# The last step of a convolution with max pooling, cut into two half steps in banks of their own

## The chip, the cores and the metric

The kernel runs on one core of a Trainium2 chip. The core has five engines that run side by side, each through its own queue in order: PE (matrix products), DVE (vector), ACT (scalar), POOL (also called GpSimd) and SP (which only issues transfers here). PE writes its sums to PSUM, which has eight banks of 512 fp32 values in each of 128 partitions; DVE and ACT read and write PSUM too, POOL does not. The metric is the time of one execution in device microseconds. The time before is the median of 3 runs, 103.41 us (103.34 to 104.08).

## The reference

A 3x3 convolution with padding 1, from 64 to 128 channels, over 16 images of 64x64, and then a maximum over windows of 2x2:

```python
batch, c_in, h, w, c_out, k = 16, 64, 64, 64, 128, 3
conv[b, co] += weight[co, ci, kh, kw] * x_pad[b, ci, kh:kh+h, kw:kw+w]   # over ci, kh, kw
output[b, c, i, j] = np.max(conv[b, c, i*2:(i+1)*2, j*2:(j+1)*2])
```

## The kernel before, in words

**Tiles.** Two images lie side by side in the 128 partitions (64 channels each), as eight tiles `xb` in bf16 with a row of zeros at the top and the bottom. Every matmul uses only the 64 rows of one image, so that two matmuls, one for each image (`h` = 0 and 1, the two lanes), run in the two halves of the array at the same time. `product` (L241) collects the products of both lanes and issues them in pairs, pass by pass. The work is cut into 32 steps: a step is a quarter of a pair of images, 16 rows of the image, that is R = 8 pairs of rows. One step and one lane fill a bank of 512 values for the upper rows of the pairs (`ta`) and another bank for the lower rows (`tb`).

**Products.** A product is three passes, one for each column of the filter (`taps`, L179): the middle one 8x64 = 512 columns wide, the outer two 8x63 = 504. With g0, g1, g2 the rows of the filter, x0 and x1 the two image rows of a pair, and x-1 and x2 the rows around it, steps come in two types:

- K steps: `ta` gets PA1 = (g2-g1) x1 and PA2 = g0 x-1, `tb` gets PB1 = (g0-g1) x0 and PB2 = g2 x2. What both rows have in common, PR = g1 (x0+x1), is added after the maximum over the two rows. Five products, 15 passes.
- W steps (all but 0, 1, 3, 5, 9 and 15, and so the last one, step 31): P2 = GM e goes into `ta`, with e = x0-x1 and GM = (g0+g2-g1)/2, and ACT copies it to `tb` (SE, `seed`, L339). P0 adds g0 (x1-x-1) to `ta`, P3 adds g2 (x2-x0) to `tb`. After the maximum over tb and -ta comes the common part P1 = GP (x0+x1), GP = (g0+g1+g2)/2. Four products, 12 passes, and a copy.

The sums and differences of rows are made beforehand in bf16: S (x0+x1, L300, on DVE), E (x0-x1, L303) and D (the differences for P0 and P3, L305), the last two on DVE or POOL. An `&` makes the rows of two neighbouring steps in one instruction, a `+` takes the other engine.

**After the products**, for each step and lane: EV (`evac`, L328) copies `ta`, negated in W steps, to SBUF on ACT; MX (`rowmax`, L344) takes the maximum of `tb` and that copy on DVE, in place; P1 or PR is added by PE; OD (`odd`, L351) copies the odd columns to SBUF on ACT; CM (`colmax`, L359) takes the maximum of even and odd columns on DVE and, when both lanes are there, issues the output. `OD+` leaves OD out: CM then reduces both columns in one instruction.

**The order** is written out by hand in `ORDER` (L429): one word for each operation, name, step, lane, and it is issued word by word, so each engine's queue follows it. `BANKS` (L483) names the bank that each start of a sum takes, in that order. An operation waits for whatever it depends on; a bank is guarded as a whole, so that a product that writes to one half of a bank waits for a reader of the other half.

**The start.** While the weights load, eight matmuls on constants (L491) keep PE busy. Then the filter rows are made into blocks (g0, g1, g2, D2, D0 and later GM, GP), each is turned by PE transposes (TD2, TG2, ..., `turn`, L136) and copied back to SBUF (VD2, VG2, ..., `turn_out`, L146) by DVE or ACT; u words (`ring`, L122) copy one slot of a block. X words cast the image's rows, L words (`load`, L315) load rows by POOL's own transfers. Step 0 is done in half steps (F, `first_product`, L256), since its rows arrive in two parts. POOL's work is held behind the DVE instruction on SBUF that stands before it (`on_gpsimd`, L70).

**The end before.** Step 31 is a W step. P2, P0 and P3 are whole, and from EV on everything is done in two halves of four pairs of rows (fourth number in the word: `P1.31.0.1` is the second half of lane 0), both halves in the same two banks. The last words are P1.28.0 and CM.28.0. Outputs behind the last operation of ACT are issued by SP and ACT in turn.

Of the kernel before, what the change touches and what calls it, by code (L numbers as in the profile page):

```python
# [11 lines left out]
def kernel(  # L12
# [9 lines left out]
    nc = tc.nc  # L22
# [59 lines left out]
    def span_of(part=None):  # L82
        return (0, R) if part is None else (0, R // 2) if part == 0 else (R // 2, R)
# [95 lines left out]
    def taps(t, h, m0, rows, start=False, skip=None, span=(0, R)):  # L179
        lo = h * CI  # L180
        i0, i1 = span
        if skip == i0:
            i0 += 1
        if skip == i1 - 1:
            i1 -= 1

        def one(kw):
            o0, o1, c0, c1 = (0, W, 0, W) if kw == 1 else (1, W, 0, W - 1) if kw == 0 else (0, W - 1, 1, W)
            if start and kw == 1:
                unset.discard(t)  # L190
            nc.tensor.matmul(  # L191
                acc[:, t, i0:i1, o0:o1],
                wt[lo : lo + CI, tap_of(m0, kw, h), :],
                rows(lo, i0, i1, c0, c1),
                start=start and kw == 1,
                stop=True,
                skip_group_check=True,
            )

        return [lambda kw=kw: one(kw) for kw in (1, 0, 2)]  # L200
# [11 lines left out]
    def rows_at(s):  # L212
        p, q = place[s]
        return xb[p], 2 * R * q + 1
# [5 lines left out]
    def top(s):  # L220
        return 0 if place[s][1] == 0 else None

    def bottom(s):
        return R - 1 if place[s][1] == NQ - 1 else None

    PRODUCTS = {
        "PA1": lambda s, h: taps(take(ta, s, h), h, D2, of_x(s, 1), start=True),
        "PA2": lambda s, h: taps(ta[s, h], h, G0, of_x(s, -1), skip=top(s)),
        "PB1": lambda s, h: taps(take(tb, s, h), h, D0, of_x(s, 0), start=True),
        "PB2": lambda s, h: taps(tb[s, h], h, G2, of_x(s, 2), skip=bottom(s)),  # L230
        "PR": lambda s, h, *part: taps(tb[s, h], h, G1, step1(row["s", s]), span=span_of(*part)),
        "P2": lambda s, h: taps(take(ta, s, h), h, GM, step1(row["e", s]), start=True),
        "P0": lambda s, h: taps(ta[s, h], h, G0, step2(row["d", s], 0)),
        "P3": lambda s, h: taps(tb[s, h], h, G2, step2(row["d", s], 1)),
        "P1": lambda s, h, *part: taps(tb[s, h], h, GP, step1(row["s", s]), span=span_of(*part)),
# [5 lines left out]
    def product(name, s, h, *part):  # L241
        lanes[h].append((name, s, h, *part))
        while lanes[0] and lanes[1]:
            a, b = (PRODUCTS[n](*args) for n, *args in (lanes[0].popleft(), lanes[1].popleft()))
# [11 lines left out]
    def first_product(k, part):  # L256
# [6 lines left out]
        pair_of_taps(where, s, m0, of_x(s, shift), start, skip, span_of(part))  # L263
# [41 lines left out]
    def row_d(s, alt):  # L305
        row["d", s] = d_pool.tile([128, 2 * R, W], BF16, name="d")
        t, f = rows_at(s)
        engine, note = (nc.vector, on_vector) if alt else (nc.gpsimd, on_gpsimd)
        note(
            engine.tensor_tensor(  # L310
                out=row["d", s], in0=t[:, f + 1 : f + 1 + 2 * R, :], in1=t[:, f - 1 : f - 1 + 2 * R, :], op=SUB
# [16 lines left out]
    def evac(s, h, *part, alt):  # L328
# [3 lines left out]
        if TYPES[s] == "K":  # L332
# [11 lines left out]
    def rowmax(s, h, *part):  # L344
        i0, i1 = span_of(*part)
# [5 lines left out]
    def odd(s, h, *part, alt):  # L351
# [3 lines left out]
        i0, i1 = span_of(*part)  # L355
# [3 lines left out]
    def colmax(s, h, *part, free):  # L359
        i0, i1 = span_of(*part)  # L360
        o = tile_of(ot, o_pool, s, WO, "o")
        t = acc[:, tb[s, h], i0:i1]
        if (s, h) in direct:
            nc.vector.tensor_reduce(  # L364
                out=o[:, h], in_=t.rearrange("p r (w two) -> p r w two", two=2), axis=mybir.AxisListType.X, op=MAX
# [3 lines left out]
        if part == (0,):  # L369
            return  # L370
        made.setdefault(s, []).append(h)
        p, q = place[s]
        dst = out[2 * p : 2 * p + 2, :, q * R : (q + 1) * R, :].rearrange("b c h w -> c b (h w)")
        src = o.rearrange("p b h w -> p b (h w)")
        queue = nc.sync
        if free:
            queue = (nc.scalar, nc.sync)[(free + 1) % 2]
# [28 lines left out]
    for m in PRODUCTS:  # L406
        steps[m] = lambda *args, m=m: product(m, *args)
    either = {
        "GS": outer_sum, "D": row_d, "SE": seed,
# [12 lines left out]
    for m in ("G0", "G1", "G2"):  # L422
# [7 lines left out]
        D2 g2 TD2 TG2 g0 D0 XOa+ g1+ TD0 XEa+ TG0 VD2 GS VD0 VG2 VG0+ uG1+ F.0.0 F.2.0 F.1.0 L.0.49.64 XEb+  # L430
        TG1 XOb+ VG1 F.3.0 L.1.0.17 F.3.1 GM uGM+ GP F.0.1 S.0 X1+ F.1.1 uGP+ F.2.1 EV.0.1 L.1.17.33 PA1.1.0
        TGM X2 X3 EV+.0.0 L.1.33.64 PB1.1.0 MX.0.1 MX.0.0 PA2.1.0 PR.0.0 TGP PA1.1.1 X4 PB1.1.1 PR.0.1 PA2.1.1
        PA1.3.0 PB2.1.0 S.1 VGM+ VGP+ PB1.3.0 PB2.1.1 EV.1.1 EV.1.0 PA1.5.0 OD+.0.1 PA2.3.0 PA1.3.1 CM.0.1
        PB1.3.1 L.2.0.33 OD+.0.0 PA2.3.1 PB2.3.1 CM.0.0 PA2.5.0 MX.1.1 EV.3.1 MX.1.0 L.2.33.64 EV.3.0 S&.3
        PB2.3.0 D+.2 PR.1.1 OD.1.1 PA1.5.1 PB1.5.0 S.2 EV.5.0 MX.3.1 E&.4 PR.3.1 PR.1.0 MX.3.0 L.3.0.64 P2.4.1
        OD.3.1 PB2.5.0 PA2.5.1 SE.4.1 PR.3.0 OD.1.0 CM.1.1 D+.4 P0.4.1 P2.4.0 S.4 P3.4.1 EV.5.1 OD.3.0 E+.6
        MX.5.0 EV.4.1 P2.2.1 SE.4.0 CM.1.0 CM.3.0 CM.3.1 P2.6.1 MX.4.1 PR.5.0 P2.6.0 OD.5.0 SE.2.1 E+.7 P0.4.0
        P3.4.0 P1.4.1 P0.2.1 CM.5.0 D+.6 SE.6.0 EV.4.0 P0.6.0 P3.2.1 SE.6.1 S&.8 S&.7 D+.7 P0.6.1 P3.6.0
        EV.2.1 MX.4.0 EV.6.0 E+.8 MX.2.1 L.4.0.64 MX.6.0 P3.6.1 EV.6.1 OD.4.1 PB1.5.1 PB2.5.1 PA1.9.0 P1.4.0
        CM.4.1 P2.7.0 P1.2.1 P1.6.0 MX.6.1 D.8 OD.4.0 P1.6.1 PA2.9.0 SE.7.0 CM.4.0 MX.5.1 D.10 OD.6.0 OD.2.1  # L440
        P2.7.1 P0.7.0 EV.9.0 CM.2.1 PR.5.1 CM.6.0 P3.7.0 OD+.6.1 P2.8.1 EV.7.0 SE.7.1 P0.7.1 P3.7.1 P2.8.0
        CM.6.1 OD.5.1 MX.7.0 PB1.9.0 CM.5.1 SE.8.0 E&.10 SE.8.1 P0.8.1 P2.10.1 P1.7.0 P3.8.1 EV.7.1 S&.10
        MX.7.1 OD.7.0 L.5.0.64 D.14 P0.8.0 P1.7.1 PB2.9.0 CM.7.0 EV.8.0 P3.8.0 SE.10.1 EV.8.1 MX.9.0 MX.8.0
        P0.10.1 P2.2.0 PR.9.0 SE.2.0 MX.8.1 S&.12 P3.10.1 P1.8.0 OD.7.1 P1.8.1 OD.9.0 PA1.9.1 OD.8.0 PA1.15.1
        PA2.9.1 CM.7.1 P0.2.0 P3.2.0 CM.9.0 EV.10.1 EV.2.0 P2.10.0 CM.8.0 MX.10.1 PA1.15.0 E&+.12 MX.2.0
        P1.2.0 OD.8.1 CM.8.1 SE.10.0 PA2.15.1 PA2.15.0 EV.9.1 OD.2.0 PB1.9.1 D+.13 D+.11 CM.2.0 S&.17 P1.10.1
        D+.12 P2.11.0 EV.15.1 EV.15.0 PB2.9.1 P0.10.0 E+.14 P2.12.1 SE.11.0 EV.10.0 OD.10.1 P3.10.0 P2.11.1
        P0.11.0 MX.9.1 MX.10.0 S&.18 SE.12.1 EV.11.0 PR.9.1 P3.11.0 P0.12.1 P1.10.0 P2.12.0 CM.10.1 SE.11.1
        OD.9.1 MX.11.0 OD.10.0 P3.12.1 CM.9.1 EV.12.1 P1.11.0 P0.11.1 SE.12.0 OD.11.0 E&+.18 CM.10.0 MX.12.1
        P3.11.1 P2.13.0 D+.16 EV.11.1 SE.13.0 P1.12.1 P0.12.0 P3.12.0 D+.19 EV.12.0 OD.12.1 CM.11.0 MX.11.1  # L450
        P2.14.1 CM.12.1 P0.13.0 SE.14.1 P3.13.0 P2.13.1 MX.12.0 EV.13.0 P0.14.1 P2.14.0 P3.14.1 E&+.16 SE.13.1
        EV.14.1 SE.14.0 P1.11.1 P1.12.0 P0.13.1 MX.13.0 P3.13.1 P1.13.0 S&.20 S&.15 OD.13.0 L.6.0.64 MX.14.1
        EV.13.1 CM.13.0 P1.14.1 P2.17.1 P0.14.0 P3.14.0 PB1.15.1 EV.14.0 MX.13.1 PB1.15.0 OD.12.0 D.17 OD.14.1
# [94 lines left out]
```

## Time and profile before

| | before |
|---|---|
| median of 3 runs | 103.41 us (103.34 to 104.08) |
| the profiled execution | 103.55 us |
| its span, from the first instruction to the last | 101.8 us |
| mean granted clock of PE | 0.98 |
| matmuls | 867: 8 on constants, 25 transposes, 834 on L191 |
| transfers | 18.02 MB, 177 GB/s on the mean |

The profile is one execution, taken by the hardware's profiler. Engines are busy while an instruction runs. PE's matmuls overlap: the next one starts before the result of the last is there, so that a matmul's own duration (0.38 us for 512 columns) is longer than the time from one to the next. In the groups, `64*128 64x512` is a matmul with 64 rows of weights, 128 columns of them, over 512 columns. `acc` is the whole PSUM, `d`, `e`, `s`, `ev`, `od`, `o` are the tiles of the operations above, `wq` and `wt` the filter blocks before and after the turn. A time behind `<-` is idle time of the engine just before the instruction, with what ended it.

### The profile page before, as it was taken

The page shows a single profiled execution, that of the slowest core. Times are in us where ns is not written, and L with a number is a line of the kernel's source. Part 1 is how long each engine was busy: PE and PEld are TensorE (multiplying, and loading weights), DVE is VectorE, ACT ScalarE, POOL GpSimd, SP SyncE. Part 2 cuts the span into 40 slices and gives each one's busy share as a digit, 9 for nine tenths or more (in the row PEclk, how much of TensorE's full clock was granted, in tenths as well). Part 3 has the DMA queues.
Part 4 walks back from the last instruction along what each step waited for, and adds up shares of the span by engine and source line. Part 5 has one row for each costly group of instructions (what it writes and reads, how often), then busy time and mean ns, then how long its engine had stood idle before and what let it go on. Part 6 is the DMA issues. An engine that isn't in the chain of part 4 may idle for free.

```text
span 101.8 us, 2430 instructions
## 1 busy us (share of the span) xinstructions
PE 95.1 (93%) x867; PEld 54.5 (54%) x867; DVE 91.7 (90%) x200; ACT 83.3 (82%) x186; POOL 56.7 (56%) x44
## 2 busy tenths in 40 slices
PE   6999999999999999999999999999999999998610
PEld 2477444545566666675565555667565555544300
DVE  3559999999999999999999999899999999999640
ACT  5567647889898979999869999999999899988320
POOL 2072502535986752647597568776678997580000
PEclk9999999999999999999999999999999999999965
DMA  2999999999999999870289790879892350420063
GB/s 44 352 327 179 141 186 199 230 234 222 271 227 169 279 259 214 277 248 6 26 132 202 208 354 13 148 155 176 235 333 95 113 206 1 170 90 0 4 231 125
DMA packets 11035, 18.02 MB, mean 177 GB/s; under 512 B 784, under 2 KB 9104, under 8 KB 10384
## 3 DMA queue, kind: packets, MB, share of 16 engines
q0 software_dynamic: 1584, 7.59, 42.2%
q1 hardware_dynamic: 9296, 10.16, 29.3%
q8 instruction: 6, 0.10, 0.4%
q10 hardware_dynamic: 144, 0.13, 0.4%
q14 instruction: 5, 0.04, 0.1%
HBM read 17.07 MB, written 8.39 MB: 250 GB/s over the span
## 4 chain that ended last, share of the span: by engine, by line
PE 92%; DVE 2%; ACT 1%; issue 0%; DVEq 0%
PE acc L191 87%; PE acc L492 4%; PE acc L140 2%; DVE o L368 1%; ACT od L357 1%; DVE acc L347 1%; DVEq L368 0%; DVEq L347 0%
## 5 line engine op out<-in xcount | busy, mean ns | idle before, releaser
L191 PEld LDWEIGHTS <-wt 64*128 64x128 bf16 x834 | 51.5, 94 | 38.6 <-issue 5.5
L191 PE MATMUL acc<-d,wt 64*128 64x504 bf16 (+1 forms) x312 | 62.6, 377 | 0.0
L191 PE MATMUL acc<-s,wt 64*128 64x504 bf16 (+3 forms) x198 | 45.6, 370 | 1.2 <-DVE o L368 0.5
L347 DVE TENSOR_TENSOR acc<-acc,ev 128x512 f32<-128x512 f32 (+1 forms) x66 | 43.4, 678 | 1.2 <-ACT ev L337 0.5
L191 PE MATMUL acc<-e,wt 64*128 64x512 bf16 (+1 forms) x156 | 39.0, 376 | 0.0
L342 ACT COPY acc<-acc 128x512 f32<-128x512 f32 x52 | 30.5, 587 | 3.4 <-PE acc L191 1.4
L310 POOL TENSOR_TENSOR d<-xb 128x1024 bf16<-128x1024 bf16 x13 | 27.7, 2131 | 6.1 <-PE acc L191 2.2
L337 ACT ACTIVATE ev<-acc 128x512 f32<-128x512 f32 (+1 forms) x53 | 30.7, 591 | 0.5 <-PE acc L191 0.2
L297 POOL TENSOR_TENSOR e<-xb 128x1024 bf16<-128x1024 bf16 (+1 forms) x13 | 21.8, 1680 | 12.1 <-DVE d L310 8.8
L191 PE MATMUL acc<-xb,wt 64*128 64x512 bf16 (+7 forms) x168 | 22.9, 344 | 0.0
L357 ACT COPY od<-acc 128x256 f32<-128x256 f32 (+1 forms) x55 | 19.5, 373 | 4.1 <-PE acc L191 2.7
L368 DVE TENSOR_TENSOR o<-acc,od 128x256 f32<-128x256 f32 (+1 forms) x55 | 21.3, 407 | 1.6 <-PE acc L191 1.1
L316 POOL DMA_DIRECT2D xb<-in_x_dram x11 | 6.2, 562 | 12.1 <-DVE e L297 4.6
L297 DVE TENSOR_TENSOR s<-xb 128x1024 bf16<-128x1024 bf16 (+1 forms) x18 | 11.3, 636 | 0.0
L310 DVE TENSOR_TENSOR d<-xb 128x1024 bf16<-128x1024 bf16 x13 | 8.8, 692 | 0.0
L333 ACT COPY ev<-acc 128x512 f32<-128x512 f32 x11 | 6.3, 592 | 2.7 <-PE acc L191 2.6
L364 DVE TENSOR_REDUCE o<-acc 128x256 f32<-128x512 f32 x11 | 7.4, 686 | 0.1
L492 PE MATMUL acc<-const-bfloat16-1.0 128*128 128x512 bf16 x8 | 3.6, 625 | 0.8 <-PEq L529 0.8
L172 POOL TENSOR_TENSOR gsum<-wraw 128x192 f32<-128x192 f32 x1 | 0.8, 809 | 3.8 <-DVE wq L164 3.8
L140 PEld LDWEIGHTS <-wq 128*128 128x128 bf16 x25 | 2.0, 122 | 1.2 <-DVE wq L397 0.8
L158 DVE COPY wt<-acc 128x512 bf16<-128x512 bf16 (+1 forms) x4 | 1.5, 403 | 1.1 <-PE acc L140 1.1
L140 PE MATMUL acc<-ident,wq 128*128 128x128 bf16 x25 | 2.5, 262 | 0.0
(28 smaller groups left out, 17.5 us busy)
## 6 DMA issues: line engine op xcount, KB each, us to landing
out_dram<-o SPq DMA_DIRECT2D x31, 256.0 KB, 6.3
xb<-in_x_dram POOLq DMA_DIRECT2D x5, 1024.0 KB, 11.0
xb<-in_x_dram POOLq DMA_DIRECT2D x2, 496.0 KB, 9.1
xb<-in_x_dram POOLq DMA_DIRECT2D x1, 528.0 KB, 8.7
ksecond<-in_x_dram SPq DMA_DIRECT2D x1, 512.0 KB, 5.5
kthird<-in_x_dram SPq DMA_DIRECT2D x1, 512.0 KB, 6.2
wraw<-in_weight_dram SPq DMA_DIRECT2D x1, 288.0 KB, 3.0
kfirst<-in_x_dram SPq DMA_DIRECT2D x1, 288.0 KB, 3.2
```

The source lines that it names most:

```text
L140: nc.tensor.transpose(tp[:, (j - lo) * CO : (j - lo + 1) * CO], wq[:, j : j + 2, :].rearrange("a b c -> a (b c)"), ident,)
L191: nc.tensor.matmul(acc[:, t, i0:i1, o0:o1], wt[lo : lo + CI, tap_of(m0, kw, h), :], rows(lo, i0, i1, c0, c1), start=start and kw == 1, sto ...
L297: note(engine.tensor_tensor(out=dst, in0=in0, in1=in1, op=op))
L310: engine.tensor_tensor(out=row["d", s], in0=t[:, f + 1 : f + 1 + 2 * R, :], in1=t[:, f - 1 : f - 1 + 2 * R, :], op=SUB)
L333: (nc.vector.tensor_copy if alt else nc.scalar.copy)(out=dst, in_=src)
L337: nc.scalar.mul(dst, src, -1.0)
L342: (nc.vector.tensor_copy if alt else nc.scalar.copy)(out=acc[:, t], in_=acc[:, ta[s, h]])
L347: nc.vector.tensor_tensor(out=t, in0=t, in1=ev[s][:, h, i0:i1], op=MAX)
L357: nc.scalar.copy(out=dst, in_=acc[:, tb[s, h], i0:i1, 1::2])
L364: nc.vector.tensor_reduce(out=o[:, h], in_=t.rearrange("p r (w two) -> p r w two", two=2), axis=mybir.AxisListType.X, op=MAX)
L368: nc.vector.tensor_tensor(out=o[:, h, i0:i1], in0=t[:, :, 0::2], in1=od[s][:, h, i0:i1], op=MAX)
L492: nc.tensor.matmul(acc[:, n].rearrange("p a b -> p (a b)"), ones[:, 0:128], ones, start=True, stop=True, skip_group_check=True)
```

## The change

Step 31 becomes two half steps, 31 and 32, both on the same quarter of the image. `quarter(s)` gives the place of a step, `span_of(s)` the rows of it: all eight pairs for steps below 31, the first four for 31, the last four for 32. The fourth number in the words is gone.

- Step 31 stays a W step, with all of its products and its copies half as wide.
- Step 32 is done without a common part left for later: `ta` gets PA1, PA2 and PRA, `tb` gets PB1, PB2 and PRB, six products and 18 passes, each half as wide. There is no EV, MX or OD for it; CM.32 takes the maximum over both banks and both columns in one reduction.
- Steps 31 and 32 have banks of their own, and so has each lane.
- The output of a step is issued when both lanes are there, now for step 28 too, whose lanes went out one by one. The last output is the first half of the quarter, 128 partitions x 2 images x 128 values, on ACT's queue.
- The order of all words is new, and so is the string of banks, 139 starts instead of 135. At the start D2 is DVE's second instruction, VD2, VG1 and VGM go to ACT, XEa and the sum g0+g2 (GS) to DVE, the turn of G1 comes ahead of that of D0, and the loads of the second pair come ahead of the last rows of the first. Of 26 D words DVE does 8 instead of 13, POOL 18 instead of 13; of the E words DVE does 8 instead of 3, POOL 8 instead of 13.

```diff
+    def quarter(s):
+        return min(s, N - 1)
+
+    def half_of(part):
+        return (0, R // 2) if part == 0 else (R // 2, R)
+
+    def span_of(s):
+        return (0, R) if s < N - 1 else half_of(s - (N - 1))
...
-    def taps(t, h, m0, rows, start=False, skip=None, span=(0, R)):
+    def taps(t, h, m0, rows, start=False, skip=None, span=(0, R), whole=True):
...
+    def first_taps(where, s, h, m0, rows):
+        return taps(take(where, s, h), h, m0, rows, start=True, span=span_of(s), whole=s < N - 1)
...
+        "PA1": lambda s, h: first_taps(ta, s, h, D2, of_x(s, 1)),
+        "PA2": lambda s, h: taps(ta[s, h], h, G0, of_x(s, -1), skip=top(s), span=span_of(s)),
+        "PRA": lambda s, h: taps(ta[s, h], h, G1, step1(row["s", quarter(s)]), span=span_of(s)),
+        "PB1": lambda s, h: first_taps(tb, s, h, D0, of_x(s, 0)),
+        "PB2": lambda s, h: taps(tb[s, h], h, G2, of_x(s, 2), skip=bottom(s), span=span_of(s)),
+        "PRB": lambda s, h: taps(tb[s, h], h, G1, step1(row["s", quarter(s)]), span=span_of(s)),
...
     def seed(s, h, alt):
+        i0, i1 = span_of(s)
         t = take(tb, s, h)
         assert t not in unset
-        (nc.vector.tensor_copy if alt else nc.scalar.copy)(out=acc[:, t], in_=acc[:, ta[s, h]])
+        (nc.vector.tensor_copy if alt else nc.scalar.copy)(out=acc[:, t, i0:i1], in_=acc[:, ta[s, h], i0:i1])
...
-    def colmax(s, h, *part, free):
-        i0, i1 = span_of(*part)
+    def colmax(s, h, free):
+        i0, i1 = span_of(s)
         o = tile_of(ot, o_pool, s, WO, "o")
         t = acc[:, tb[s, h], i0:i1]
+        if s == N:
+            a, b = sorted((ta[s, h], tb[s, h]))
+            nc.vector.tensor_reduce(
+                out=o[:, h, i0:i1],
+                in_=acc[:, a : b + 1 : b - a, i0:i1].rearrange("p k r (w two) -> p r w k two", two=2),
+                axis=mybir.AxisListType.XY,
+                op=MAX,
+            )
...
-        if s == LAST:
-            queue.dma_start(out=dst[:, h : h + 1], in_=src[:, h : h + 1])
-        elif len(made[s]) == 2:
-            queue.dma_start(out=dst, in_=src)
+        queue = (nc.sync, nc.sync, nc.scalar)[free % 2 + 1 if free else 0]
+        queue.dma_start(out=dst, in_=o[:, :, i0:i1].rearrange("p b h w -> p b (h w)"))
...
     ORDER = """
-        D2 g2 TD2 TG2 g0 D0 XOa+ g1+ TD0 XEa+ TG0 VD2 GS VD0 VG2 VG0+ uG1+ F.0.0 F.2.0 F.1.0 L.0.49.64 XEb+
-        TG1 XOb+ VG1 F.3.0 L.1.0.17 F.3.1 GM uGM+ GP F.0.1 S.0 X1+ F.1.1 uGP+ F.2.1 EV.0.1 L.1.17.33 PA1.1.0
+        g2+ g1 D2 g0 TG2 TD2 uG1+ XOa+ TG1 VD2+ VG2 D0 XOb+ GS+ XEa XEb+ X2 TD0 L.1.0.17 TG0 VD0 L.1.17.33
+        VG0+ F.0.0 GP uGP+ F.2.0 F.0.1 F.3.1 GM F.1.0 S.0 X1+ F.1.1 EV+.0.1 EV.0.0 F.3.0 F.2.1 VG1+ uGM+
...
-        P3.30.0 P1.30.1 P0.31.0 EV.30.0 MX.30.0 OD+.30.1 SE.31.1 EV.31.0.0 CM.30.1 P0.31.1 P3.31.1 EV.31.0.1
-        P3.31.0 EV.31.1.0 P1.29.1 MX.31.0.0 P1.30.0 MX.31.0.1 MX.31.1.0 EV.31.1.1 P1.31.0.0 MX.31.1.1 OD.30.0
-        OD.31.0.0 OD.29.1 P1.31.1.0 CM.31.0.0 CM.30.0 P1.31.0.1 OD.31.0.1 OD.31.1.0 P1.31.1.1 P1.28.0 CM.29.1
-        CM.31.1.0 CM.31.0.1 OD.31.1.1 OD.28.0 CM.31.1.1 CM.28.0
+        CM.26.1 MX.29.0 P2.30.1 P1.27.0 P2.29.1 P1.29.0 EV.28.1 CM.27.1 SE.28.0 OD.27.0 E+.31 MX.28.1 CM.27.0
+        OD+.29.0 SE.30.1 P1.28.1 CM.29.0 P0.28.0 P0.30.1 P2.30.0 EV.28.0 P3.28.0 OD+.28.1 P3.30.1 SE.29.1
+        P0.29.1 P2.31.0 P3.29.1 CM.28.1 SE.30.0 EV.30.1 EV.29.1 P0.30.0 D+.31 S&.30 P3.30.0 P2.31.1 MX.28.0
+        EV.30.0 SE.31.0 MX.30.1 MX.29.1 P1.28.0 P1.30.1 MX.30.0 P0.31.0 SE.31.1 OD.28.0 P0.31.1 P3.31.1
+        CM.28.0 P3.31.0 P1.29.1 EV.31.0 P1.30.0 MX.31.0 PB1.32.0 PA1.32.1 EV.31.1 OD.30.1 CM.30.1 PB1.32.1
+        P1.31.0 PRA.32.1 PA1.32.0 PB2.32.0 OD.30.0 PRB.32.0 MX.31.1 OD.31.0 OD.29.1 PRB.32.1 CM.30.0 PB2.32.1
+        CM.31.0 PA2.32.1 PRA.32.0 CM.29.1 P1.31.1 PA2.32.0 CM.32.1 CM.32.0 OD.31.1 CM.31.1
     """
```

More of the change, by code (lines that the diff above doesn't have):

```diff
@@ L189, in one @@
             if start and kw == 1:
-                unset.discard(t)
+                (unset.discard if whole else unset.add)(t)
             nc.tensor.matmul(
@@ L220, in top @@
     def top(s):
-        return 0 if place[s][1] == 0 else None
+        return 0 if place[quarter(s)][1] == 0 else None
     def bottom(s):
-        return R - 1 if place[s][1] == NQ - 1 else None
+        return R - 1 if place[quarter(s)][1] == NQ - 1 else None
+    def first_taps(where, s, h, m0, rows):
+        return taps(take(where, s, h), h, m0, rows, start=True, span=span_of(s), whole=s < N - 1)
     PRODUCTS = {
-        "PA1": lambda s, h: taps(take(ta, s, h), h, D2, of_x(s, 1), start=True),
@@ L228 @@
[L228 to L233, printed above, removed]
@@ L236, with product @@
+        "P1": lambda s, h: taps(tb[s, h], h, GP, step1(row["s", quarter(s)]), span=span_of(s)),
     }
     lanes = (deque(), deque())
-    def product(name, s, h, *part):
-        lanes[h].append((name, s, h, *part))
+    def product(name, s, h):
+        lanes[h].append((name, s, h))
         while lanes[0] and lanes[1]:
-            a, b = (PRODUCTS[n](*args) for n, *args in (lanes[0].popleft(), lanes[1].popleft()))
+            a, b = (PRODUCTS[n](s_, h_) for n, s_, h_ in (lanes[0].popleft(), lanes[1].popleft()))
@@ L262, in first_product @@
             take(where, s, 1)
-        pair_of_taps(where, s, m0, of_x(s, shift), start, skip, span_of(part))
+        pair_of_taps(where, s, m0, of_x(s, shift), start, skip, half_of(part))
     pair_tiles = {}
@@ L310, in row_d @@
             engine.tensor_tensor(
[L311 removed]
+                out=row["d", s][:, 0:n, :], in0=t[:, f + 1 : f + 1 + n, :], in1=t[:, f - 1 : f - 1 + n, :], op=SUB
             )
@@ L349, with odd @@
     direct = set()
-    def odd(s, h, *part, alt):
+    def odd(s, h, alt):
         if alt:
@@ L406 @@
     for m in PRODUCTS:
-        steps[m] = lambda *args, m=m: product(m, *args)
+        steps[m] = lambda s, h, m=m: product(m, s, h)
     either = {
-        "GS": outer_sum, "D": row_d, "SE": seed,
+        "GS": outer_sum, "D": row_d, "SE": seed, "EV": evac, "OD": odd,
         "XOa": lambda alt: cast_first(1, MID, alt),
@@ new lines @@
+        L.2.0.33 S.1 L.2.33.64 OD+.0.1 PA2.1.1 CM.0.1 EV.1.0 PB2.1.1 S.3 PB1.3.1 PA1.3.0 PB1.3.0 MX.1.0
+        PA1.3.1 EV.1.1 OD.0.0 L.3.0.64 PA2.3.0 TGM MX.1.1 PR.1.1 PR.1.0 CM.0.0 PB2.3.1 PA2.3.1 S.2 OD.1.1
+        PB2.3.0 D+.2 E&.2 CM.1.1 VGM EV.3.0 OD+.1.0 TGP P2.4.1 PA1.5.0 CM.1.0 MX.3.0 PA1.5.1 PB1.5.0 EV.3.1
+        PA2.5.1 PA2.5.0 PR.3.0 SE.4.1 MX.3.1 D.4 VGP+ P0.4.1 PB2.5.0 P2.2.1 S.4 P3.4.1 EV.5.0 P2.4.0 PR.3.1
+        S.5 E&.6 S&.7 EV.5.1 EV.4.1 OD.3.0 P2.6.0 SE.2.1 MX.5.0 L.4.0.64 CM.3.0 PR.5.0 SE.4.0 P0.2.1 P3.2.1
```

132 lines of the change are left out of this document (59 added, 73 removed).

## The prediction

> **What bounds the kernel now.** I read the page's head first, then busy time by stretches, then the chain of waits, and last the groups with shapes kept apart.
>
> ```profile
> span 101.8 us, 2430 instructions
> ...
> PE 95.1 (93%) x867; PEld 54.5 (54%) x867; DVE 91.7 (90%) x200; ACT 83.3 (82%) x186; POOL 56.7 (56%) x44
> ```
> ```profile
> 40.00:50.00 10.00, 10.00 (x93) 6.26 (x90) 10.00 (x20) 9.53 (x22) 5.95 (x4) 1.00 0.46 150
> ```
>
> Shares over the span would say that PE has 7% to give. The stretch says otherwise: in a stage of 10 us PE and DVE are both busy for all of it and ACT for 9.53. So the middle is full, and what is not full lies at the two ends. The chain shows them (start, length, what, how many):
>
> ```profile
> 4.35 1.58 PE acc L140 x16
> ...
> 7.25 1.75 PE acc L191 x30
> 9.00 0.44 PE acc L140 x6
> 9.44 82.12 PE acc L191 x747
> ...
> 94.80 0.28 ACT od L357
> ...
> 95.10 0.30 DVE o L368
> ...
> 95.44 0.53 PE acc L191 x6
> ...
> 96.45 0.63 PE acc L191 x3
> ```
>
> Up to 91.56 the chain is PE alone. From about 93.5 it hops between engines: passes, odd columns, column maximum, passes again. The row by row view gives the edges of the full part and the end:
>
> ```profile
> 9.37 1.68 PE L191 MATMUL acc<-xb,wt 64*128 64x512 bf16 x13
> ```
> ```profile
> 93.36 0.38 PE L191 MATMUL acc<-d,wt 64*128 64x504 bf16 x1
> ...
> 97.18 1.32 DVE L368 TENSOR_TENSOR o<-acc,od 128x128 f32<-128x128 f32 x4 [1.12 <-PE acc L191]
> ```
>
> PE's last full pass starts at 93.36; the last DVE result is there at 97.18 + 1.32 = 98.50; the span ends 3.3 us later (issue of the output, landing, closing barrier). These three stretches are my terms: head, stream, tail.
>
> **The change, part by part.**
>
> *Tail, what goes.* Before, both halves of step 31 share a bank, so P1 of the second half cannot start while the first half is read. The waits say so:
>
> ```profile
> PE acc L191 <- DVE o L368: 0.5, 1, 0.5
> PE acc L191 <- DVE acc L347: 0.4, 1, 0.4
> PE acc L191 <- ACT od L357: 0.3, 1, 0.3
> ```
>
> From 93.36 to 98.50 are 5.14 us, in which PE has only three more products to issue (18 passes; 0.65 for one with a full lane, 0.33 for halves, 1.6 together). After, step 32 has banks 6, 4, 1 and 3, whose last readers are EV.31.0, CM.30.1, EV.31.1 and CM.28.0; none is the other half.
>
> *Stream, what is added.* Step 31 had 18 full matmuls and 12 half ones. Now there are 24 half ones for step 31 and 36 for step 32: 30 matmuls more, all half. The two row lanes run together, so I count pairs. Before, 128 full products in pairs lie between 9.37 and 93.36, three passes each: 383 steps in 83.99 us, 0.2193 a step, with the small stalls of this order in it. Without a stall it is (1.68 - 0.38) / 6 = 0.217, by the row at 9.37, whose 13 matmuls are six steps on two lanes and the first of the next. Half passes are those of the first step: the chain's 30 in 1.75 us are 0.117 a pair with some gaps, and half of 0.217 is 0.109; I take 0.11. From start to result one takes 0.27:
>
> ```profile
> L191 PE MATMUL acc<-xb,wt 64*128 64x252 bf16 x28 | 2.4, 270 | 0.0
> ```
>
> In the new order 127 pairs of products are paced by a full lane (two mix a full one with a half one) and 9 are half on both lanes. 381 x 0.2193 = 83.55 and 27 x 0.11 = 2.97, together 86.52. I keep the stalls of before in it, 383 x (0.2193 - 0.217), some 1 us: both orders alternate the same kinds of steps with the same eight banks, and DVE's work after the head is about equal (two half maxima and five D fewer; five E, two reductions and some smaller ones more). That is the largest unknown; bounds below.
>
> *Head.* D2 is now DVE's second instruction, VD2 goes to ACT, three transposes of G1 come ahead of TD0, and GS leaves GpSimd. Rows of before:
>
> ```profile
> 4.16 0.49 DVE L398 TENSOR_TENSOR wq<-wraw 128x192 bf16<-128x192 f32 x1
> 4.98 0.41 DVE L158 COPY wt<-acc 128x512 bf16<-128x512 bf16 x1
> 5.74 0.76 DVE L158 COPY wt<-acc 128x512 bf16<-128x512 bf16 x2 [0.35 <-PE acc L140]
> ```
> ```profile
> 5.37 0.59 ACT L156 COPY wt<-acc 128x512 bf16<-128x512 bf16 x1
> ```
>
> The second turn is read at 5.37 before; D2's takes that place now, so VD2 is 5.37 to 5.96 and F.0.0 starts at 5.98; before, the chain goes on with it at 4.35 + 1.58 = 5.93. Three transposes (0.1 each, 1.58 / 16) put VD0 from 5.74 to about 5.95, done 6.36, so F.2.0 starts at 6.40. Seven products at 0.34 follow without a TG1 or a wait between: 8.78. TGM and TGP (0.44 in the chain) come later and still count: 9.22 stands against 9.37, a gain of 0.15. If VD2 is late by one ACT instruction, it is a loss of 0.3; if F.2.0 does not wait, a gain of 0.35.
>
> *New tail.* Stream end 9.22 + 86.52 = 95.74. The last pass starts 0.11 earlier and takes 0.27, so PE's last result is there at 95.90. What runs behind it:
>
> ```profile
> L364 DVE TENSOR_REDUCE o<-acc 128x256 f32<-128x512 f32 x11 | 7.4, 686 | 0.1
> L347 DVE TENSOR_TENSOR acc<-acc,ev 128x256 f32<-128x256 f32 x4 | 1.6, 430 | 0.2
> L337 ACT ACTIVATE ev<-acc 128x256 f32<-128x256 f32 x4 | 1.3, 381 | 0.2 <-PE acc L191 0.2
> ```
>
> CM.32.1 reads as many elements as the reduction of L364 (two banks of 256 for 512) and its banks are done one product earlier, at 95.6; 0.69. DVE starts an instruction some 0.08 before the one ahead of it is over (4.16 to 4.98 above holds two of 0.49), so CM.32.0 runs 96.2 to 96.9, and CM.31.1 (0.30) 96.8 to 97.1. OD.31.1 (0.28, from 95.9) is hidden by CM.32.0; without that cover it would stand on the path itself. Nothing in the trace reduces across two banks: its price lies between 0.43 (a 256 instruction, if both banks came side by side) and 1.37 (twice 0.69); I take 0.69, the row with the same count. Only one of the two lies on the path, so -0.3 to +0.9. The cover of P1.31.0: counted from the start of P0.31, P0.31 and P3.31 are there at 0.5 and 0.8, EV.31.0 (0.38) ends at 0.9 and MX.31.0 (0.43) at 1.3, and its place in PE's order is 1.64 (two half products and a full one, 0.33 + 0.33 + 0.65, and PB1.32): 0.3 of slack. PA1.32.0 stands a third of a microsecond later and waits for CM.30.1, which follows MX.31.0 and OD.30.1 on DVE and is over at 1.8. Thin, but positive; if the first is gone, P1.31 waits and all behind it with it.
>
> The last transfer keeps its size, in 256 pieces of 512 B instead of 128 of 1 KB:
>
> ```profile
> out_dram<-o ACTq DMA_DIRECT2D x1, 128.0 KB, 2.2
> ```
>
> No row has such pieces on this path. Shorter than before it cannot be, since the bytes are the same and the pieces more; twice the pieces at the same price each would at most add 1.1, half of the 2.2 again, as if all of it were pieces. I leave the 3.3 us as they are, since the bytes stay.
>
> *Work moved between DVE and GpSimd.* Five D's go from DVE to GpSimd, and five e's come back. Each engine's sum changes by under 1.5 us, but they must not meet:
>
> ```profile
> 34.03 0.79 DVE L297 TENSOR_TENSOR s<-xb 128x1024 bf16<-128x1024 bf16 x1
> ```
> ```profile
> 32.12 2.14 POOL L310 TENSOR_TENSOR d<-xb 128x1024 bf16<-128x1024 bf16 x1
> ```
> ```profile
> L347 DVE TENSOR_TENSOR acc<-acc,ev 128x512 f32<-128x512 f32 x62 | 41.7, 694 | 1.0 <-ACT ev L337 0.5 <-PE acc L191 0.2
> L310 POOL TENSOR_TENSOR d<-xb 128x1024 bf16<-128x1024 bf16 x13 | 27.7, 2131 | 6.1 <-PE acc L191 2.2
> L368 DVE TENSOR_TENSOR o<-acc,od 128x256 f32<-128x256 f32 x51 | 20.3, 416 | 0.2
> L297 DVE TENSOR_TENSOR s<-xb 128x1024 bf16<-128x1024 bf16 x14 | 9.6, 697 | 0.0
> L297 POOL TENSOR_TENSOR e<-xb 128x512 bf16<-128x512 bf16 x6 | 6.9, 1160 | 7.9 <-DVE d L310 6.7 <-DVE s L297 1.1
> ```
>
> S&.12 started 0.23 before D.14 was over and took 0.79, where its group needs 0.70: a meeting cost 0.1. The Trainium skill, SBUF — State Buffer, section "Who interferes with whom", speaks for more: a DVE instruction with two SBUF inputs and a GpSimd instruction that reads SBUF exclude each other for the whole instruction, whoever is first. By that rule one early meeting would put up to GpSimd's whole 2.1 us on the sum; the trace shows only this late meeting, which neither proves nor denies it. By the row a meeting is worth 0.1, less than I can count here, and I add nothing.
>
> **Sum.** 97.1 + 3.3 = 100.4 of span. Around the span lie 103.55 - 101.8 = 1.75, so 102.1 for a profiled run; that run was 0.14 above the median of 103.41, so 102.0.
>
> **Rivals.**
>
> *No stalls* (0.15). The new order drops the 1 us of stalls kept in the stream, and the head gains its 0.35 instead of 0.15. For: the stretch shown has no PE idle at all, so the stalls are an accident of places. 102.0 - 1.2 = 100.8.
>
> *The gain goes into the middle* (0.16). GpSimd gets a chain behind S&.27: D.29, D.28, E.30, D.30, E.31, that is 3 x 2.13 + 2 x 1.16 = 8.7 us, and DVE has 8.3 of work until its next instruction on SBUF (eight of 0.694, three of 0.686 and five of 0.416, each less 0.08). Counted from the start of P0.31: MX.30.0 starts at -0.5 and DVE has 11.6 us of work from S&.27 to there, so S&.27 is over at -11.4 and D.28, second in the chain, at -7.1. Its product P0.28 stands eleven pairs before P0.31, 11 x 0.65 = 7.1: no room at all. If the chains come late by 0.6 each (this one and the one of 8.5 us behind E&.18), PE waits for them: 102.0 + 1.2 = 103.2. Against: before has a chain of four behind S&.28, 7.6 us against 6.7 of DVE's work, and its stream still came out at 0.2193.
>
> *The end is not as short* (0.08). Reduction at twice the price and slow pieces: +0.9; 102.9.
>
> *Slower* (0.11). DVE's S, E and D meet GpSimd early and are shut out whole. Two meetings of 2.1 us, at the two chains over 8 us (behind E&.18 and behind S&.27), on a DVE that has no idle time in the stretch shown, reach PE undiminished: 106.2. It decides from 2.4 us on. Against: the mean of this kind over all fourteen is 0.697. This is the rule of the Trainium skill's page on SBUF named above, and no row here shows it.
>
> My forecast has 0.50.
>
> **How the numbers follow.** One per cent is about what a measurement of this kernel can tell from no change; the bounds are 102.4 and 104.4. Of the forecast's 0.50 some 0.40 lie below 102.4 (0.4 of room against the head's 0.3 and the reduction), the rest between. Faster 0.40 + 0.15 = 0.55; within 1% 0.10 + 0.16 + 0.08 = 0.34; slower 0.11. The range goes from 100.9, which cuts half of the no-stall case, to 104.0, which cuts the slower one: just under 0.2 outside.
>
> **What would show it.** First full pass about 8.8, with the two turns after it. PE's last pass near 95.6, no wait of PE on DVE or ACT over 0.2 in the last 4 us. Reductions of 128x128 out at 0.69. From PE's last result to DVE's last 1.2 us. Wrong it is if the full pairs take over 0.2193 us a step, and the releaser then names which rival: "DVE d", "POOL d" or "POOL e" for the GpSimd chain, S, E or D of DVE over 0.8 us for the meetings.

## The result and the profile after

| | before | after |
|---|---|---|
| median of 20 runs each | 103.85 us (103.24 to 104.54) | 103.33 us (102.77 to 104.15) |
| the profiled execution | 103.55 us | 103.78 us |
| its span | 101.8 us | 102.0 us |
| matmuls | 867 | 897 |

The ratio of the times is 0.9947, with a 95% interval of 0.9921 to 0.9972: half a per cent faster, where I had forecast 1.4%. The profiled execution of the changed kernel is one of its slower ones, 0.45 us over its median, so I profiled the same kernel once more (run after_again below) before I counted in tenths. First the profile that came with the result. The head of its page, and the same stretch of 10 us as before (span of the stretch, PE, PE's weight loads, DVE, ACT, POOL, granted clock, DMA share, GB/s):

```profile
span 102.0 us, 2471 instructions
...
PE 95.7 (94%) x897; PEld 59.5 (58%) x897; DVE 91.2 (89%) x199; ACT 82.3 (81%) x182; POOL 56.7 (56%) x43
```
```profile
40.00:50.00 10.00, 10.00 (x92) 5.04 (x90) 9.80 (x19) 9.35 (x21) 6.37 (x5) 1.00 0.96 201
```

PE is still busy for all of it. DVE, which had no gap here before, now has 0.20. The chain of waits of the changed kernel (start, length, what, how many):

```profile
1.19 4.70 DMA kfirst<-in_x_dram
5.90 0.02 issue
5.92 0.41 ACT xb L401
6.33 0.49 ACT wt L162
...
16.86 80.13 PE acc L197 x749
96.99 0.02 issue
97.01 1.29 DVE o L378 x2
98.30 0.20 DVEq L555
```

Two things are to be seen. The tail that hopped between PE, DVE and ACT is gone: PE alone leads up to 96.99, then come the two reductions. And at the other end the chain begins with the first rows of the image: they landed at 5.89 (before 4.43), ACT cast them at 5.92 and only then copied the turned block at 6.33. That is XOa standing ahead of VD2 in ACT's queue. The last operations on DVE, and what SP waited for in all (line, releaser: sum, times, longest), the last two rows being the closing barrier on L555:

```profile
95.36 1.00 DVE L389 TENSOR_TENSOR o<-acc,od 128x256 f32<-128x256 f32 x3
97.01 1.29 DVE L378 TENSOR_REDUCE o<-acc 128x128 f32<-128x512 f32 x2 [0.65 <-PE acc L197]
98.22 0.28 DVE L389 TENSOR_TENSOR o<-acc,od 128x128 f32<-128x128 f32 x1
```
```profile
SPq L396 <- DVE o L389: 75.5, 25, 11.2
SPq L396 <- DVE o L385: 7.0, 5, 2.4
SPq L555 <- DMA out_dram<-o: 1.5, 2, 1.2
SPq L555 <- PEq L555: 1.1, 2, 0.5
```

PE's last result is there at 96.98, since its last row in the trace is this one:

```profile
96.71 0.27 PE L197 MATMUL acc<-s,wt 64*128 64x252 bf16 x1
```

DVE stood idle for 0.65 and began CM.32.1 at 97.01, behind PE's last result of all; forecast was a start 0.3 ahead of it. And in the barrier SP waited 1.1 us; before, the same two rows were these:

```profile
SPq L543 <- DMA out_dram<-o: 1.8, 2, 1.4
...
SPq L543 <- SPq L543: 0.4, 1, 0.4
SPq L543 <- PEq L543: 0.2, 1, 0.2
```

Together 2.6 us after and 2.4 before, though the last transfer itself lands sooner. In the trace's records of semaphores one step of POOL in this barrier, from its first record there to its next, takes 0.44 after and 0.08 before.

### The profile page after: what moved, and what is told of

The parts are those of the page before. It is cut to its first block, busy times and chain, and to the rows that moved or that the text cites. A ratio compares the mean times of both kernels' runs of the same rounds, so it can differ in the third digit from the quotient of the medians.

```text
span 102.0 us, 2471 instructions
## 1 busy us (share of the span) xinstructions
PE 95.7 (94%) x897; PEld 59.5 (58%) x897; DVE 91.2 (89%) x199; ACT 82.3 (81%) x182; POOL 56.7 (56%) x43
## 4 chain that ended last, share of the span: by engine, by line
PE 88%; DMA 5%; DVE 1%; ACT 1%; SPq 0%; issue 0%; DVEq 0%
PE acc L197 88%; DMA kfirst<-in_x_dram 5%; DVE o L378 1%; PE acc L146 1%; ACT wt L162 0%; ACT xb L401 0%; SPq L81 0%; DVEq L555 0%
## 5 line engine op out<-in xcount | busy, mean ns | idle before, releaser
L197 PEld LDWEIGHTS <-wt 64*128 64x128 bf16 x864 | 56.2, 94 | 33.1 <-issue 4.2
L197 PE MATMUL acc<-d,wt 64*128 64x504 bf16 (+3 forms) x312 | 63.4, 373 | 0.0
L322 POOL TENSOR_TENSOR d<-xb 128x1024 bf16<-128x1024 bf16 x18 | 38.1, 2129 | 17.1 <-DVE s L308 9.0
L197 PE MATMUL acc<-s,wt 64*128 64x504 bf16 (+3 forms) x204 | 47.2, 367 | 0.0
L197 PE MATMUL acc<-e,wt 64*128 64x512 bf16 (+2 forms) x156 | 38.2, 372 | 0.0
L355 ACT COPY acc<-acc 128x512 f32<-128x512 f32 (+1 forms) x52 | 29.6, 576 | 3.5 <-PE acc L197 2.3
L197 PE MATMUL acc<-xb,wt 64*128 64x504 bf16 (+6 forms) x192 | 27.2, 333 | 0.5 <-ACT wt L162 0.5
L308 POOL TENSOR_TENSOR e<-xb 128x512 bf16<-128x512 bf16 (+1 forms) x8 | 12.2, 1523 | 5.3 <-PE acc L197 2.7
L308 DVE TENSOR_TENSOR e<-xb 128x1024 bf16<-128x1024 bf16 (+1 forms) x8 | 5.2, 649 | 0.0
L322 DVE TENSOR_TENSOR d<-xb 128x1024 bf16<-128x1024 bf16 (+1 forms) x8 | 5.2, 647 | 0.0
```

Source lines behind the costliest of these rows:

```text
L197: nc.tensor.matmul(acc[:, t, i0:i1, o0:o1], wt[lo : lo + CI, tap_of(m0, kw, h), :], rows(lo, i0, i1, c0, c1), start=start and kw == 1, sto ...
L308: note(engine.tensor_tensor(out=dst, in0=in0, in1=in1, op=op))
L322: engine.tensor_tensor(out=row["d", s][:, 0:n, :], in0=t[:, f + 1 : f + 1 + n, :], in1=t[:, f - 1 : f - 1 + n, :], op=SUB)
```

## The experiments

My theory after the result had two places in it, both small: the wait of CM.32.1, and the closing step. A rival was that the new order of the middle costs PE what the end saves, and another that the head (a cast ahead of the turned block) does. Eleven runs told them apart; the first four on one chip, the others on a second one, each beside the kernel before.

**e1_banks: other banks at the end.** CM.32.1 reads banks 1 and 3 in one instruction. Bank 2 between them belongs to lane 1 of step 31, and its P1.31.1 is PE's very last product. The two SE of step 31 exchange their banks, so that bank 5 is the one that is late, and OD.31.1 goes ahead of CM.32.0:

```diff
-        ... PA2.32.0 CM.32.1 CM.32.0 OD.31.1 CM.31.1
+        ... PA2.32.0 CM.32.1 OD.31.1 CM.32.0 CM.31.1
-        "745632071634025674123706153427601526314"
+        "745632071634025674123706153427601256314"
```

> The changed kernel with SE.31.0 and SE.31.1 in each other's banks (5 and 2), and OD.31.1 ahead of CM.32.0. Theory A (a wait on a bank that lies between the two banks of the reduction): CM.32.1 starts 0.3 us before PE's last result instead of 0.03 behind it, DVE is done 1.2 us behind PE instead of 1.5, and the time falls by 0.35 us, to 0.991 of before where the changed kernel is 0.995. Rival (the reduction waits for its own passes, and the bank between them is no matter): CM.32.1 still starts behind PE's last result, ratio 0.995.

Measured: 103.25 us, ratio 0.9951 (0.9919 to 0.9982). The operations of DVE at the end, and PE's last matmul:

```profile
94.91 1.00 DVE L389 TENSOR_TENSOR o<-acc,od 128x256 f32<-128x256 f32 x3
96.24 1.32 DVE L378 TENSOR_REDUCE o<-acc 128x128 f32<-128x512 f32 x2 [0.33 <-PE acc L197]
97.47 0.28 DVE L389 TENSOR_TENSOR o<-acc,od 128x128 f32<-128x128 f32 x1
```
```profile
96.26 0.27 PE L197 MATMUL acc<-s,wt 64*128 64x252 bf16 x1
```

Now the reduction starts 0.29 before PE's last result (96.24 against 96.26 + 0.27 = 96.53), and DVE ends 1.22 behind PE instead of 1.52. So the wait was for the bank between the two that are read, not for the data: 0.3 us. (OD.31.1 stands behind CM.32.1 in either order and has no part in this wait.) The exchange is not free: ACT's copies for step 31 (SE) now start 0.12 to 0.15 later, counted from the first full pass, and PE's last result comes 0.12 later. From the first full pass to DVE's end the four profiles with the old banks (the changed kernel twice, e2, e6) take 88.94 to 88.96 us, the three with the exchanged banks (e1, e12, e7) 88.76 to 88.78. So 0.18 of the 0.3 reaches the end. The time alone does not show so small a step here, and the expected 0.991 did not come.

**e2_turn_first: the cast behind the turned block.** XOa+ moves behind VD2+ on ACT.

```diff
-        ... TD2 uG1+ XOa+ TG1 VD2+ VG2 ...
+        ... TD2 uG1+ TG1 VD2+ XOa+ VG2 ...
```

> The changed kernel with XOa+ behind VD2+ on ACT instead of ahead of it. Theory A (the cast waits for the first rows, and the copy of the turned weights waits behind it): where the first rows land at 5.9 us as in the profile of the changed kernel, F.0.0 starts at 6.35 instead of 6.87 and the time falls by 0.5 us, to 0.990 of before; where they land at 4.4 as in the profile of before, F.0.0 starts at 6.2 instead of 6.0 and 0.2 us is lost. Rival (the middle is full on DVE as on PE, so a head start is lost in stalls): F.0.0 is earlier but PE's last pass stands where it stood, ratio 0.995.

Measured: 103.31 us, ratio 0.9971 (0.9941 to 1.0). Here the first rows landed early, at 4.44, and ACT's row shows what the move costs then:

```profile
5.40 0.58 ACT L162 COPY wt<-acc 128x512 bf16<-128x512 bf16 x1 [0.51 <-PE acc L146]
5.88 0.41 ACT L401 CAST xb<-kfirst 128x256 bf16<-128x256 f32 x1
```

The cast now waits for the turn and the first product starts at 6.34; in either order the one behind waits for the one ahead. Nothing is won on the mean.

**e12_both: both edits.**

```diff
-        ... TD2 uG1+ XOa+ TG1 VD2+ VG2 ...
+        ... TD2 uG1+ TG1 VD2+ XOa+ VG2 ...
-        ... CM.32.1 CM.32.0 OD.31.1 CM.31.1
+        ... CM.32.1 OD.31.1 CM.32.0 CM.31.1
-        "745632071634025674123706153427601526314"
+        "745632071634025674123706153427601256314"
```

> Both edits of the two runs before. Theory A: the two places are far apart in time, so the two gains add, 0.35 + 0.5 = 0.85 us with late rows, ratio 0.987, and 0.15 us with early ones, 0.994. Rival (full middle): 0.995 or, if only the end counts, 0.991.

Measured: 103.31 us, ratio 0.9953 (0.9919 to 0.9987); DVE again ends 1.22 behind PE, span 101.4. The two together are no more than the first.

**e5_tail_alone: the new end on the old order.** Order and banks of the kernel before up to P3.30.0, and behind it the two half steps, with neighbouring banks for step 32 (3 and 4, 6 and 7), so that none lies between:

```diff
-        P3.30.0 P1.30.1 P0.31.0 EV.30.0 ... CM.31.1.1 CM.28.0
+        P3.30.0 P1.30.1 P1.28.0 EV.30.0 MX.30.0 OD+.30.1 SE.31.1 OD.28.0 P0.31.0 P0.31.1 P3.31.1 P3.31.0 CM.28.0
+        CM.30.1 EV.31.0 P1.30.0 P1.29.1 MX.31.0 EV.31.1 PB1.32.0 PA1.32.1 PB1.32.1 P1.31.0 PRA.32.1 PA1.32.0
+        PB2.32.0 OD.30.0 PRB.32.0 MX.31.1 OD.31.0 OD.29.1 PRB.32.1 CM.30.0 PB2.32.1 CM.31.0 PA2.32.1 PRA.32.0
+        CM.29.1 P1.31.1 PA2.32.0 CM.32.1 OD.31.1 CM.32.0 CM.31.1
```

> The old order and the old banks up to step 30, with the new end alone: step 31 as half step, step 32 with 18 passes and one reduction, in banks of their own (3 and 4, 6 and 7, none in between). Theory A (the end was worth what the prediction said, and the new head gave part of it back): PE starts P0.31 at about 92.3, DVE is done about 5.1 us later, 1.1 us earlier than before: ratio 0.989, better than the changed kernel. Rival (the 30 added half passes eat the gain of the end, and the new order earned the rest): 1.000, worse than the changed kernel.

Measured: 102.55 us, ratio 0.986 (0.9808 to 0.9912), clear of e1 on the same chip (0.9919 to 0.9982). The end alone gives what I had forecast for the whole. Its rows of the end and of the barrier:

```profile
96.30 1.29 DVE L378 TENSOR_REDUCE o<-acc 128x128 f32<-128x512 f32 x2 [0.26 <-PE acc L197]
97.50 0.28 DVE L389 TENSOR_TENSOR o<-acc,od 128x128 f32<-128x128 f32 x1
```
```profile
SPq L551 <- DMA out_dram<-o: 1.5, 4, 0.6
...
SPq L551 <- SPq L551: 0.4, 1, 0.4
SPq L551 <- PEq L551: 0.2, 1, 0.2
```

The reductions start ahead of PE's last result (96.59) here too, and the barrier takes 2.1 us, not 2.6. In this kernel POOL still makes the sum g0+g2 (GS); in the changed one DVE does, and POOL's program is three records shorter (74 against 77 in the trace; GS accounts for two of them, as e8 shows below). That made the next theory: the closing step depends on POOL's program, not on its work.

**after_again: the changed kernel once more**, with no edit.

> The changed kernel once more, on the same chip as the three that follow. With first rows that land at 4.4 to 5.0 us, as in four of the five profiles of this start so far, F.0.0 starts at 5.9 and the first full pass at 9.0, DVE is done at 98.1 and the span is 101.6: closing of 3.5 us behind DVE's last result, against 3.3 and 3.1 in the two profiles of the old order. Ratio 0.995. Rival (late rows are what is usual here): first full pass at 9.5 again and a span of 102.

Measured: 102.95 us, ratio 0.9928 (0.9897 to 0.996), span 101.2. Its chain of waits:

```profile
0.78 3.57 PE acc L506 x8
4.35 1.93 PE acc L146 x19
6.28 7.19 PE acc L197 x90
...
16.07 80.13 PE acc L197 x749
96.20 0.02 issue
96.23 1.29 DVE o L378 x2
```

The long piece is the same to the hundredth, 80.13 for 749 passes, and everything is 0.79 earlier. So what was slow in the first profile lay ahead of the first full pass (9.54 there, 8.77 here): the rows landed at 5.89 there and at 5.00 here, and with them came the cast that the turned block stands behind.

**e6_filler: POOL's program longer by three instructions.** Three memsets of one column each, into a tile that nobody reads, right behind the constants at the start:

```diff
+    spare = const.tile([128, 4], FP32)
+    for n in range(3):
+        nc.gpsimd.memset(spare[:, n : n + 1], 0.0)
```

> The changed kernel with three memsets of 128x1 on GpSimd at the start, into a tile that nobody reads, so that GpSimd's program is as long as before or a little longer. Theory A (one step of the closing barrier on GpSimd takes 0.42 us instead of 0.08 where its program is shorter than before, since its last instructions then lie otherwise in what is fetched): the step takes 0.08 again, the closing falls by 0.35 us, ratio 0.9915. Rival (the step depends on the order of the work or on the last transfers): still 0.42, ratio 0.995.

Measured: 102.99 us, ratio 0.9908 (0.9874 to 0.9942). The barrier:

```profile
SPq L558 <- DMA out_dram<-o: 1.5, 3, 0.7
...
SPq L558 <- SPq L558: 0.4, 1, 0.4
SPq L558 <- PEq L558: 0.2, 1, 0.2
```

2.1 us instead of 2.6, POOL's step 0.08 instead of 0.42, and 3.18 us from DVE's end to the span's end instead of 3.48. More instructions at the start, less time at the end: the profile shows that the step depends on what stands in POOL's program, though the times of the two kernels alone (102.95 and 102.99) would not.

**e7_banks_filler: e1 and e6 together.**

```diff
-        ... CM.32.1 CM.32.0 OD.31.1 CM.31.1
+        ... CM.32.1 OD.31.1 CM.32.0 CM.31.1
-        "745632071634025674123706153427601526314"
+        "745632071634025674123706153427601256314"
+    for n in range(3):
+        nc.gpsimd.memset(spare[:, n : n + 1], 0.0)
```

> The changed kernel with the exchanged banks of step 31 and OD.31.1 ahead of CM.32.0, and the three memsets. Theory A: both gains, 0.3 us at the reduction and 0.35 us in the closing, ratio 0.988 to 0.989. Rival: the time does not follow the profile's end, 0.995.

Measured: 102.48 us, ratio 0.9886 (0.984 to 0.9931), span 100.4. With both repairs the new order gains 1.1%, near the forecast. On this chip that is 0.5 us off the changed kernel, as 0.18 from the banks and 0.3 from the close would have it; the intervals still overlap, but the profile shows both steps: 97.26 to 100.44 at the close, 1.22 from PE to DVE. That its span is the forecast 100.4 to the tenth is luck: its first full pass stands at 8.48, 0.3 earlier than was forecast.

**e8_tail_gs: e5 with the sum on DVE.**

```diff
-        ... XEa+ TG0 VD2 GS VD0 VG2 VG0+ ...
+        ... XEa+ TG0 VD2 GS+ VD0 VG2 VG0+ ...
```

> The old order with the new end alone, and the sum g0+g2 on DVE instead of GpSimd, as the changed kernel has it: GpSimd's program is one operation shorter. Theory A: the step of the closing barrier takes 0.42 us as in the changed kernel and the span is 0.35 us longer than the 100.9 of the new end alone; ratio 0.9895 where the new end alone had 0.986. Rival: the step stays at 0.08, ratio 0.986.

Measured: 102.01 us, ratio 0.9827 (0.9794 to 0.986), the lowest of all. So the expected 0.42 did not come: POOL's step stayed at 0.08 with 75 records; between 74 and 75 it changes. Whether GS was worth a third of a per cent I then asked by itself.

**e9_before_gs: the kernel before, with that one word changed**, and with it **e5_again** and **e8_again**, the two kernels once more, without an edit:

```diff
-        ... XEa+ TG0 VD2 GS VD0 VG2 VG0+ ...
+        ... XEa+ TG0 VD2 GS+ VD0 VG2 VG0+ ...
```

> The kernel before with the sum g0+g2 on DVE instead of GpSimd and nothing else. Theory A (the new end earns what the old order with it shows; this edit only fills a pause of 0.35 us that DVE has there): 1.000 of before, at most 0.2 us faster by the first load of GpSimd leaving earlier. Rival (the head of the changed kernel is what earns, by this part of it): 0.996 or less.

> The old order with the new end alone, a second time. Theory A: 0.986 again, DVE done 1.2 us behind PE's last result and a closing of 3.1 to 3.2 us. Rival (the first measurement was a lucky one and the end is worth no more than the whole change): 0.993.

> The old order with the new end and the sum on DVE, a second time, beside the new end alone on the same chip. Theory A: the sum on DVE is worth 0 to 0.2 us, so 0.984 to 0.986, and this or the run beside it is the fastest of all versions. Rival (the sum on DVE is worth the 0.5 us that lay between their first measurements): 0.981 beside 0.986.

Measured: e9 103.71 us, ratio 1.0015 (0.9983 to 1.0047); e5 again 102.24 us, 0.9876 (0.9836 to 0.9916); e8 again 102.29 us, 0.9881 (0.9844 to 0.9919). GS is worth nothing that the times show, and e8's first 0.9827 was not found again. (In the profiles e8 is 0.2 us shorter than e5 from the first full pass to P0.31, both times, and 0.1 longer in the close.) What stands is that the new end on the old order, in four measurements between 0.9827 and 0.9881, beats both kernels of this case, and that the new order of head and middle adds nothing to it.

**What the middle costs.** From the starts of the products in the traces I took the stretch from the first full pass to P0.31, without the two turns in it. The changed kernel has 126 pairs of products there in 82.97 us, 0.6585 a pair (0.2195 a pass); before had 125 in 82.19, 0.6575 (0.2192); e5 126 in 82.65 and e8 in 82.44. Against before, the new order is neutral to 0.1 us; against the same end on the old order it costs 0.3 to 0.5 us. The waits of PE's weight loads hint at where, first in the first profile of the changed kernel, then in e5_again:

```profile
PEld L197 <- ACT acc L355: 1.2, 4, 0.3
...
PEld L197 <- DVE o L389: 0.4, 1, 0.4
PEld L197 <- ACT ev L349: 0.3, 1, 0.3
```
```profile
PEld L197 <- DVE d L322: 0.3, 1, 0.3
PEld L197 <- DVE wt L164: 0.3, 1, 0.3
PEld L197 <- DVE o L389: 0.2, 1, 0.2
```

In the new order it is the copies of SE on ACT, four times, that PE stands behind; the loads run ahead, so the 1.2 us are more than PE itself loses. I made no run that moves these copies, so that they are the cause of the 0.3 to 0.5 is read from the waits and not shown.

## Why the prediction was wrong in size

The time lies in the range and the direction held, but 0.5% was measured where 1.4% was said. Two steps failed: the start of the last reductions and the closing barrier. The table loses 0.8 of the forecast 1.4 us; the 0.6 that are left agree with the measured half per cent. By steps, forecast against the second profile of the changed kernel, times from the span's start:

| step | forecast | measured | late by then |
|---|---|---|---|
| first full pass | 8.78 | 8.77 | 0.0 |
| two turns behind it | 0.44 | 0.55 | 0.1 |
| P0.31, 126 pairs at 0.2193 a pass | 92.1 | 92.27 | 0.2 |
| PE's last result | 95.90 | 96.19 | 0.3 |
| DVE's last result | 97.1 | 97.71 | 0.6 |
| span | 100.4 | 101.2 | 0.8 |

*Head, stream: right in size, in part by luck.* The full pass came at the time said in this profile. In the five profiles with this head it came between 8.48 and 9.54, 8.90 on the mean, and with the 0.55 of the two turns that is 9.45. The six profiles with the old head (three of them with GS on DVE), which have their two turns ahead of the first full pass, have 9.21 to 9.86 and 9.49 on the mean. So the forecast 0.15 of the head does not show. The stalls kept in the stream came in the size that was kept, 0.2195 a pass against 0.2193, though this was called the largest unknown. By the letter of the prediction's own sign (over 0.2193) that is too much, by 0.1 us in all, and the releaser is ACT's SE, which no rival had named. In the first profile the head was 0.8 later, because XOa+ stands ahead of VD2 and the rows came late; the bounds of the head (-0.3 to +0.35) did not hold that, since I had bounded VD2 by one ACT instruction and not by the landing that the instruction waits for.

*New tail: the first step that failed.* The words "its banks are done one product earlier, at 95.6" took the two banks that CM.32.1 reads. The program guards the range from the first to the last, and the bank between them was PE's last. The row shows 0.65 of idle DVE, and the reduction starts 0.3 us later than the forecast has it against PE's last result. With two banks exchanged (e1, e7) it starts on time; 0.18 of the 0.3 then reaches the end.

*The price of the reduction: right.* Over two banks and two columns it took what the row with as many elements takes:

```profile
L378 DVE TENSOR_REDUCE o<-acc 128x128 f32<-128x512 f32 x2 | 1.3, 686 | 0.7 <-PE acc L197 0.7
```

*Last transfer and closing: the second step that failed.* "I leave the 3.3 us as they are, since the bytes stay." The pieces of 512 B did not cost. The prediction held that the transfer could not be shorter than before; it landed after 2.0, before after 2.2 (1.99 to 2.15 in the eleven profiles with these pieces, 2.18 in the two without):

```profile
out_dram<-o ACTq DMA_DIRECT2D x1, 128.0 KB, 2.0
```

But the 3.3 hold the barrier, and a step of POOL in it grew by 0.33 to 0.36 when POOL's program lost three records. In the prediction GS was only a sum that changes its engine, and the barrier's length a constant. The shorter transfer hides a part of this in the table, where the close is only 0.2 late: e5, e6, e7 and e8 show that without the long step the close takes 3.11 to 3.25, so 0.3 were lost.

The rest, 0.3, is spread over the turns, the stream and PE's last ten pairs (3.92 from P0.31 to the last result, 3.8 forecast). And the three runs of before that the prediction started from had a median of 103.41, where larger sets had 103.50 to 103.85, so that it took both kernels for 0.1 to 0.4 us faster than they are. The ratio is hardly touched by that.

*The tail that goes: right.* No wait of PE on DVE or ACT is left in the last 4 us, and the slack of 0.3 for P1.31 held. e5 isolates it, and gives 1.2 to 1.4%, the size that the forecast gave to the end together with a small gain of the head.

*Small readings.* The 93.36 called PE's last full pass is the last of the unbroken stream; full passes of one lane run until 96.68. DVE's work beside the chain of 8.7 adds up to 8.4 from its rows, not 8.3. Neither changes the sum.

*Rivals.* "No stalls" did not happen. "The end is not as short" happened, but not by the reduction's price or slow pieces; that its 102.9 is near the 102.95 of after_again is chance. "The gain goes into the middle" named POOL's chain behind S&.27; its product was not late, and against before the middle is neutral. "Slower" did not happen: the longest S, E or D of DVE over 1024 elements took 0.685, and the groups of the changed kernel are

```profile
L308 DVE TENSOR_TENSOR s<-xb 128x1024 bf16<-128x1024 bf16 x12 | 8.2, 681 | 0.0
L308 DVE TENSOR_TENSOR e<-xb 128x1024 bf16<-128x1024 bf16 x7 | 4.8, 682 | 0.0
L322 DVE TENSOR_TENSOR d<-xb 128x1024 bf16<-128x1024 bf16 x7 | 4.8, 680 | 0.0
```

They hardly met: in the whole trace a DVE instruction of this kind lies beside one of POOL three times, for 0.13 us at most, since POOL's are held until DVE's are over. The rule of the Trainium skill that I set beside it (SBUF — State Buffer, section "Who interferes with whom": the one that comes first keeps the shared port for its whole instruction, which the page says where it speaks of DVE's two-port modes) had no occasion in this kernel. But the kernel before had more than the one meeting that the prediction saw. In its trace a DVE instruction starts 0.08 to 0.23 us before a POOL one is over eight times. Up to 0.13 of overlap it takes 0.68 to 0.69, with 0.16 to 0.17 it takes 0.71 to 0.72, with 0.19 0.75, with 0.22 0.77 and with 0.23 0.79: beyond about 0.13 it loses what it overlaps. So these late meetings agree with an exclusion; an early one, on which the rival's 2.1 us rest, is in no trace of this case.

## What to carry to other kernels

An instruction that reads two buffers by a stride waited here for what lies between them too: give such pairs neighbouring buffers, or put between them one that is done early, and check that the exchange does not make another operation wait. A gain in the last microseconds should be followed up to the closing barrier, on every engine, since taking work off an engine that seems to have nothing to do with it can lengthen that. And a change that bundles an end with a whole new order is worth cutting apart: here the end alone carries all of the gain.

## What the hardware showed that I had not expected

- The closing step of POOL takes 0.42 to 0.44 us in the five profiles with 74 records of POOL (the changed kernel twice, e1, e2, e12), and 0.08 to 0.09 in the eight with 75 or 77. Three idle memsets at the start (e6) switch it. In the traces the lost third of a microsecond is not gone with 77 records, it stands elsewhere: the DRAIN that POOL issues ahead of the barrier comes 0.44 to 0.47 us behind the record before it, against 0.11 with 74 or 75, and there POOL still has work, so that nobody waits. With 75 neither place shows it; between the two lies POOL's wait for the barrier. The transfers point the same way: a fetch of instructions (8 KB) starts 0.65 to 0.96 us behind the DRAIN with 77 records (at 82.3 in e6), 1.07 to 1.17 behind the DRAIN's end with 75, and at 101.1 in the changed kernel's second profile, 0.64 behind the end of the long step. The Trainium skill, Runtime: NRT & Kernel Launch, section "Instruction fetch mechanics", says that instructions are fetched in blocks of 256 and that crossing a block's edge is mostly hidden. An edge that moves through POOL's last instructions with the length of its program, and is hidden in two of the three places, would fit all 13 profiles; but the traces do not say whose fetch it is, and no run shifted it instruction by instruction, so this cause is read and not shown.
- The first rows of the image (288 KB) landed between 4.43 and 5.89 us in the profiles, from the same first instruction, so that a place in the head that is free in one execution costs 0.8 us in another.
